# Up of a transformer block: one pair of output blocks by eight products instead of two, and three sums of h's blocks formed by GpSimd

## The chip, the cores and the metric

The kernel runs on one core of one Trainium2 chip. The metric is the device time of one execution in microseconds. Of the engines of the core, PE is TensorE (matmuls; PEld its weight loads), DVE is VectorE, ACT is ScalarE, POOL is GpSimd, and SP is the engine whose queue issues most loads. Each engine works through its own instructions in the order in which they stand, and waits for others through semaphores.

## The reference: what is computed

One block of a transformer on 512 tokens of width 2048, all in float32:

```
h = modulate(rms_norm(x, norm_mix), sh_a, sc_a)
...                                    # convolution and attention give y_conv, y_attn
x = x + g_a * (concat([y_conv, y_attn]) @ w_out)
h = modulate(rms_norm(x, norm_ffn), sh_f, sc_f)
x = x + g_f * ((silu(h @ ffn_w1) * (h @ ffn_w3)) @ ffn_w2)
```

The change lies in the last line: `h @ ffn_w1` and `h @ ffn_w3` (the weights are 2048 x 5632 each) are called Up here, the product with `ffn_w2` Down.

## The kernel before, in words

**Precision.** A float32 product is made of parts: a value is rounded to a high part (`hi`, type fp32r), and the rest is its low part (`lo`). Weights are split by a cast on ACT (`w_hi`, L1295) and a subtraction on DVE (`w_lo`, L1301). The blocks of h are split in the same way by `h_parts` (L1179 on ACT, L1180 on DVE); high and low half stand side by side in a tile `hC`, so that one matmul of 512 columns multiplies the weights' high part with both (L1309), and one of 256 columns adds the weights' low part times h's high part (L1310). `product` is eight such pairs of matmuls, one for each 128 rows of a half of the width.

**Pairs and products.** Up goes through 44 pairs u of output blocks: 128 columns of `ffn_w1` and the same of `ffn_w3`, each cut in an upper and a lower half of the width. A pair has four weight blocks of 128 x 1024: 11 and 21 of `ffn_w1`, 12 and 22 of `ffn_w3`. h is cut in four blocks `A[i, j]` of 128 x 2048 (i the half of the tokens, j the half of the width). A plain pair multiplies every weight block with two blocks of h: four steps, eight products (`plain_steps`, hC1 to hC4 for A[0,0], A[0,1], A[1,0], A[1,1]). All further pairs use a form of Strassen's scheme (`strassen_steps`): seven products, 1 to 7, of sums of weight blocks with sums of blocks of h. Product 1 takes weight block 11 with hC1, 5 takes 11 + 12 with hC5 (A[1,1] - A[1,0]), 2 takes 21 with hC2, 6 takes 11 + 12 + 22 with hC6, 3 takes 22 with a new hC3, 7 takes 12 + 22 with hC7 (A[0,0] - A[1,0]), 4 takes 21 + 11 + 12 + 22 with hC4. The weight sums are DVE additions (L1375 before, L1377 in the change, through `add`) and every product has its own split. The products gather in two banks of PSUM, x and y, and a third for product 2, and are read out by `take` (a copy on ACT and an addition on DVE, L1318 and L1319) and `more` (two additions on DVE, L1315). `PLAIN` pairs are plain, two of the 44 before. Product 4 of a pair is put behind the first two of the next pair; the first pair behind the plain ones has the order 1, 5, 2, 6, 3, 7, 4.

**The sums of blocks of h.** `h_sums(step)` is called once in each step n as long as n < 4 * PLAIN. Before, it forms the four sums on DVE at steps 1 to 4 (L1324, L1327, L1330, L1333) and splits them by `h_parts`; the plain pairs need none of them except that the old hC3 must be done with before the new is written (step 7). The sums are formed in place: A[1,1] becomes A[1,1] - A[1,0], A[1,0] becomes A[0,0] - A[1,0], and so on.

**Order.** The lists of steps are written out in `order`; a scheduler then places the instructions on the engines, so the order on an engine is not that of the code. The loop ahead of each step prepares later ones: a weight sum three steps ahead (`lead`), a split two steps ahead, the loads of a pair five steps ahead (`begin`). Loads of a pair go to the ring `raw` of four buffers when u <= PLAIN or u is a multiple of three, else to two buffers of `xy` (L1282). The four A blocks hold the four buffers of `xy`; they come free when the last reader of a block is done.

**Before and behind.** The end of the product with `w_out` gives x's second half late: A[1,0] and A[1,1] are made (`modulated`, L1191 on PE, L1195 on ACT) when the first three half steps of pair 0 are done. From step 8 * PLAIN on `gate_steps` runs beside the products: it loads rows of `ada_w`, scales them on ACT and adds them up by GpSimd's DMA queue. Down starts when Up is through; GpSimd stores each pair's result to DRAM (`store`), and Down reads them.

Of the kernel before, what the change touches and what calls it, by code (L numbers as in the profile page):

```python
# [10 lines left out]
F32 = mybir.dt.float32  # L11
# [3 lines left out]
ALU = mybir.AluOpType  # L15
# [5 lines left out]
S = 512  # L21
# [51 lines left out]
def block_kernel(ctx: ExitStack, tc: tile.TileContext, a: dict, out: bass.AP):  # L73
    nc = tc.nc
# [4 lines left out]
    def pool(name, bufs=1, stack=ctx, **kw):  # L79
        return stack.enter_context(tc.tile_pool(name=name, bufs=bufs, reuse_waits="tile", **kw))  # L80
# [443 lines left out]
    for k0 in range(0, KC, STEP):  # L524
        n = 12 if k0 == 0 else 9
# [61 lines left out]
    for name, m, t0, t1, n in (("q", 0, 0, NT, P), ("c", 1, NT, NT + 1, NP_), ("s", 2, 0, NT, P), ("w", 3, 0, NT, P)):  # L587
        f = SCALE if name == "q" else 1.0
        for h in range(2):
# [6 lines left out]
                                           op0=ALU.mult, op1=ALU.mult)  # L596
# [383 lines left out]
    HS, HK = S // 2, KC // 2  # L980
# [137 lines left out]
    A = {}  # L1118
# [3 lines left out]
    hC = {1: hc1.tile([P, HK, S], F32R, name="hC1")}  # L1122
# [44 lines left out]
    def row_norms(h):  # L1167

        r2 = rs2[:, 2 * h:2 * h + 2]
        nc.vector.reduce_sum(r2, ss2[:, 2 * h:2 * h + 2, :], axis=AX)  # L1170
        rsqrt(r2, r2, D)
        for e in range(2):
            dgs[h, e] = yp.tile([P, P], F32, tag="dn", name="dn", bufs=2)
            nc.vector.tensor_scalar(dgs[h, e], ident, rs2[:, 2 * h + e:2 * h + e + 1], None, op0=ALU.mult)

    def h_parts(p, src, k0, n):

        hi, lo = hC[p][:, k0:k0 + n, 0:HS], hC[p][:, k0:k0 + n, HS:S]
        nc.scalar.copy(hi, src)  # L1179
        nc.vector.tensor_sub(lo, src, hi.bitcast(F32))  # L1180
# [91 lines left out]
        for t in made:  # L1272
            x2_store(*t)
    row_norms(1)
    PLAIN = 2
    NU = FF // P

    def blocks(u):

        b = {}  # L1280
        for q, w, r0 in ((11, w1, 0), (21, w1, HK), (12, w3, 0), (22, w3, HK)):
            if u <= PLAIN or u % 3 == 0:  # L1282
                b[q] = ring[0].tile([P, HK * P], F32, tag="raw", name="raw")
# [37 lines left out]
    def h_sums(step):  # L1321

        if step == 1:
            nc.vector.tensor_sub(A[1, 1], A[1, 1], A[1, 0])  # L1324
            h_parts(5, A[1, 1], 0, HK)
        elif step == 2:
            nc.vector.tensor_sub(A[1, 0], A[0, 0], A[1, 0])  # L1327
            h_parts(7, A[1, 0], 0, HK)
        elif step == 3:
            nc.vector.scalar_tensor_tensor(A[0, 0], A[1, 1], -1.0, A[0, 0], op0=ALU.mult, op1=ALU.subtract)  # L1330
            h_parts(6, A[0, 0], 0, HK)
        elif step == 4:
            nc.vector.scalar_tensor_tensor(A[0, 1], A[0, 0], -1.0, A[0, 1], op0=ALU.mult, op1=ALU.subtract)  # L1333
        elif step == 4 * PLAIN - 1:
            h_parts(3, A[0, 1], 0, HK)

    def store(f, g):
        nc.gpsimd.dma_start(gd[f], g)
# [1 line left out]
    def plain_steps(u):  # L1340
        o = {}
        h = [slice(0, HS), slice(HS, S)]

        def make(q, w, j):
            def prep(s):
                s["hi"] = w_hi(o["b"][q])

            def mm(s, halves=(0, 1)):
                if j == 0 and 0 in halves:
                    o[w] = [(main, aux)[w]() for _ in range(2)]  # L1350
                for i in halves:
                    product(o[w][i], (s["hi"], s["lo"]), 1 + 2 * i + j, j == 0, j == 1)

            def post(s):
                if j == 0:
                    return
                d = o[f"d{w}"] = dp.tile([P, S], F32, tag=f"d{w + 1}", name=f"d{w + 1}")
                for i in range(2):
                    take(d[:, h[i]], o[w][i])
                if w == 0:  # L1360
                    nc.scalar.activation(d, d, AF.Silu)
                else:
                    nc.vector.tensor_mul(d, d, o["d0"])
                    store(u, d)

            return {"p": 0, "u": u, "o": o, "sum": lambda: None, "hi": prep, "src": q, "mm": mm, "post": post}

        return [make(q, w, j) for q, w, j in ((11, 0, 0), (21, 0, 1), (12, 1, 0), (22, 1, 1))]
# [68 lines left out]
    for u in range(NU):  # L1437
        new = plain_steps(u) if u < PLAIN else strassen_steps(u)
        if u == 0:
            new[1:3] = new[2], new[1]  # L1440
        if u == PLAIN:
            new[2:5] = new[4], new[2], new[3]
        order += new[:2]
        if late:
            order.append(late)
            late = None
        if u < PLAIN:
            order += new[2:]
# [8 lines left out]
    def begin(u):  # L1457
        if u < NU and u not in begun:
            begun.add(u)
            got = blocks(u)  # L1460
            for s in order:
                if s["u"] == u:
                    s["o"]["b"] = got
    def prepare(n, what):
        if n >= len(order):
            return
        s = order[n]
        if what == "sum":
            begin(s["u"])
            s["sum"]()  # L1470
        else:
            s["hi"](s)
            s["lo"] = w_lo(s["o"]["b"][s["src"]], s["hi"])
# [28 lines left out]
    def load_g(to, j, b, k):  # L1502
        to[b, k] = rings_g[j].tile([P, S], F32, tag=f"g{j}", name=f"g{j}", bufs=GM + 1)
        (nc.sync if b else nc.gpsimd).dma_start(to[b, k], gd[GROUPS[b][j][k]])
# [3 lines left out]
    for n, s in enumerate(order):  # L1508
        for m in range(n + 5, n + 1, -1):
            if m < len(order) and lead[id(order[m])] == m - n:  # L1510
                prepare(m, "sum")
        if n + 5 < len(order):
            begin(order[n + 5]["u"])
        if n > 2:
            prepare(n + 2, "split")
        if n < 4 * PLAIN:
            h_sums(n)
        s["mm"](s, (1,) if n < 3 else (0, 1)) if n < 4 * PLAIN else s["mm"](s)
        if 0 < n < 3:
            prepare(n + 2, "split")  # L1520
        s["post"](s)
        if n >= 8 * PLAIN:
            next(gate, None)
        if n == last_1:
            hst.close()
            rings_g[0] = pool("gtop", 1, side="right")
            for early in range(1, GM + 1):
                load_g(G0, 0, 0, early - 1)
# [91 lines left out]
```

## Time and profile before

| what | value |
|---|---|
| time, median of 3 runs | 2157.0 us (2156.54 to 2158.15) |
| the profiled execution | 2156.57 us |
| its span | 2154.8 us |
| Up's first product starts | 856.86 us into the span |
| Up's products with the whole of h begin | 873.07 us |
| the second pair begins | 887.33 us |
| the last weight load of L1309 | 1729.2 us |

Times in a timeline are us from the start of the span; a row has the start, the duration, the engine, the source line, what is written from what, and the shape. Where several equal instructions stand in a row, the duration is that of all of them together. Matmuls overlap: their own durations are longer than the distance between two starts, so a product is measured from start to start. `idle before` in brackets is how long the engine waited ahead of the row, and for whom.

### The profile page before, as it was taken

What the parts mean: (1) busy time and instruction counts of PE and PEld (TensorE: products, weight loads), DVE (VectorE), ACT (ScalarE), POOL (GpSimd) and SP (SyncE); (2) the same over time, 40 slices, a digit from 0 to 9 for tenths busy, and PEclk for the clock granted to TensorE, in tenths of its full rate; (3) what the DMA queues carried; (4) which work ended last, traced back from release to release, by engine and by line L of the source; (5) the groups of instructions that cost most, each with busy time, mean ns of one, the idle gap of its engine ahead of it and who ended that gap; (6) DMA issues with size and microseconds to landing.
All of it is one profiled execution on the core that took longest, in us unless ns stands there. A gap on an engine that the chain in (4) does not pass through costs nothing.

```text
span 2154.8 us, 30665 instructions
## 1 busy us (share of the span) xinstructions
PE 2125.5 (99%) x11011; PEld 1775.8 (82%) x11011; DVE 1780.1 (83%) x2776; ACT 1077.8 (50%) x1795; POOL 251.9 (12%) x336
## 2 busy tenths in 40 slices
PE   7999999999999999999999999999999999999998
PEld 5678778778788878888888888888888888888887
DVE  4998778878778789888888888888888877777888
ACT  5334345554442556655555555555555455554543
POOL 1110000000000233001100110110110140212032
PEclk9999999999999999999999999999999999999999
DMA  9984776545557999546666665665665499998897
GB/s 334 359 288 137 225 234 193 167 140 153 156 153 238 267 197 236 157 118 169 168 169 171 180 167 161 166 174 146 175 170 148 167 242 282 216 247 192 221 186 181
DMA packets 384778, 422.91 MB, mean 196 GB/s; under 512 B 21881, under 2 KB 293793, under 8 KB 383857
## 3 DMA queue, kind: packets, MB, share of 16 engines
q1 hardware_dynamic: 343216, 296.58, 44.5%
q0 software_dynamic: 41264, 124.23, 26.5%
q8 instruction: 87, 1.43, 0.3%
q14 instruction: 67, 0.54, 0.1%
q10 hardware_dynamic: 144, 0.13, 0.0%
HBM read 385.20 MB, written 19.94 MB: 188 GB/s over the span
## 4 chain that ended last, share of the span: by engine, by line
PE 87%; DVE 5%; DMA 5%; issue 2%; POOL 1%; ACT 0%; SPq 0%; DVEq 0%; POOLq 0%; ACTq 0%
PE main L1309 15%; PE main L1084 12%; PE aux L1084 12%; PE aux L1309 11%; PE main L1310 8%; PE aux L1310 6%; PE main L115 4%; PE main L117 4%; PE main L116 4%; DMA araw<-in_ada_w 3%; PE aux L888 2%; PE aux L860 2%; PE aux L115 1%; DMA t<-in_w_out 1%; PE aux L117 1%
## 5 line engine op out<-in xcount | busy, mean ns | idle before, releaser
L1309 PE MATMUL main<-hC,whi 128*128 128x512 f32 x1408 | 494.6, 393 | 0.0
L1310 PE MATMUL main<-hC,wlo 128*128 128x256 f32 x1408 | 394.4, 280 | 0.0
L1309 PE MATMUL aux<-hC,whi 128*128 128x512 f32 x1072 | 377.1, 392 | 0.0
L1309 PEld LDWEIGHTS main<-hC,whi 128*128 128x128 f32 x1408 | 263.6, 187 | 59.3 <-DVE hC L1180 0.3
L1310 PE MATMUL aux<-hC,wlo 128*128 128x256 f32 x1072 | 300.6, 280 | 0.0
L1310 PEld LDWEIGHTS main<-hC,wlo 128*128 128x128 f32 x1408 | 266.0, 189 | 0.0
L1309 PEld LDWEIGHTS aux<-hC,whi 128*128 128x128 f32 x1072 | 200.8, 187 | 44.8
L1301 DVE TENSOR_TENSOR wlo<-xy,whi 128x1024 fp32r<-128x1024 f32 x135 | 164.6, 1220 | 62.5 <-ACT whi L1295 62.5
L1310 PEld LDWEIGHTS aux<-hC,wlo 128*128 128x128 f32 x1072 | 202.6, 189 | 0.3 <-DVE wlo L1301 0.2
L1295 ACT CAST whi<-xy 128x1024 fp32r<-128x1024 f32 x135 | 142.3, 1054 | 104.6 <-issue 48.6
L1084 PE MATMUL aux<-wlo,phi 128*128 128x512 f32 (+1 forms) x422 | 164.4, 390 | 0.9 <-DVE wlo L1029 0.9
L1084 PE MATMUL main<-wlo,phi 128*128 128x512 f32 x420 | 163.7, 391 | 1.2 <-DVE wlo L1029 0.8
L1084 PE MATMUL aux<-whi,plo 128*128 128x512 f32 (+1 forms) x422 | 163.8, 388 | 0.0
L1084 PE MATMUL aux<-whi,phi 128*128 128x512 f32 (+1 forms) x422 | 163.6, 388 | 0.0
L1084 PE MATMUL main<-whi,plo 128*128 128x512 f32 x420 | 163.5, 389 | 0.0
L1084 PE MATMUL main<-whi,phi 128*128 128x512 f32 x420 | 163.5, 389 | 0.0
L1295 ACT CAST whi<-t 128x1024 fp32r<-128x1024 f32 x84 | 88.6, 1055 | 137.0 <-PE main L1309 64.3
L115 PE MATMUL main<-alo,whi 128*128 128x512 f32 x384 | 155.5, 405 | 0.0
L117 PE MATMUL main<-ahi,whi 128*128 128x512 f32 x384 | 151.4, 395 | 0.0
L116 PE MATMUL main<-ahi,wlo 128*128 128x512 f32 x384 | 150.6, 392 | 0.0
L1027 ACT CAST whi<-raw 128x1024 fp32r<-128x1024 f32 x90 | 94.7, 1054 | 111.1 <-PE aux L1084 37.8
L1027 ACT CAST whi<-xy 128x1024 fp32r<-128x1024 f32 x88 | 92.8, 1054 | 112.0 <-issue 41.1
(353 smaller groups left out, 4443.7 us busy)
## 6 DMA issues: line engine op xcount, KB each, us to landing
xy<-in_ffn_w SPq DMA_DIRECT2D x130, 512.0 KB, 4.8
raw<-in_ffn_w SPq DMA_DIRECT2D x107, 512.0 KB, 4.7
araw<-in_ada_w SPq DMA_DIRECT2D x208, 256.0 KB, 5.3
xy<-in_ffn_w POOLq DMA_DIRECT2D x66, 512.0 KB, 9.0
raw<-in_w_in SPq DMA_DIRECT2D x128, 192.0 KB, 3.2
xy<-in_ada_w SPq DMA_DIRECT2D x80, 256.0 KB, 4.0
graw<-in_ada_w SPq DMA_DIRECT2D x60, 256.0 KB, 2.8
acc<-graw POOLq DMA_DIRECT2D x60, 256.0 KB, 3.8
```

Of the source, the lines that this page charges most:

```text
L115: nc.tensor.matmul(ps, lhs[0], rhs[1], start=first, stop=False)
L116: nc.tensor.matmul(ps, lhs[1], rhs[0], start=False, stop=False)
L117: nc.tensor.matmul(ps, lhs[0], rhs[0], start=False, stop=last)
L860: nc.tensor.matmul(one[b], queries(g, i, h), kT[b][g][:, :L], start=True, stop=True)
L888: nc.tensor.matmul(po[:, b * HD:(b + 1) * HD], s["pT"][b][:, kb * P:(kb + 1) * P], vv[b][:, kb, g * HD:(g + 1) * HD], start=kb == 0, stop= ...
L1027: nc.scalar.copy(hi, wt)
L1084: nc.tensor.matmul(ps[:, q:q + wide], at_k[l][:, tok], wt[r][:, cs], start=begins and m == 0, stop=ends_ and j == i and m == 2, skip_group ...
L1295: nc.scalar.copy(hi, t)
L1301: nc.vector.tensor_sub(lo, t, hi.bitcast(F32))
L1309: nc.tensor.matmul(ps, wt[0][:, ks[k]], hC[p][:, k, :], start=first and k == 0, stop=False, skip_group_check=True)
L1310: nc.tensor.matmul(ps[:, HS:], wt[1][:, ks[k]], hC[p][:, k, 0:HS], start=False, stop=last and k == HK - 1, skip_group_check=True)
```

## The change

`PLAIN` goes from 2 to 1: pair 1 is now made of seven products instead of eight, in the order 1, 5, 2, 6, 3, 7, 4, and all later pairs move up. Since the products of pair 1 need sums of blocks of h, these are formed earlier and elsewhere: the first stays on DVE, the other three are formed by GpSimd at step 1, one behind the other. The signs change: A[0,0] becomes A[0,0] + A[1,1] (without the minus), and hC6 takes the minus when it is split, by ACT (L1332) and DVE (L1333). The splits of hC6, hC3 and hC7 are asked for at steps 4, 5 and 6. Pair 2 loads into buffers of `xy`, since u <= PLAIN no longer holds for it.

```diff
@@ -1272,7 +1272,7 @@
         for t in made:
             x2_store(*t)
     row_norms(1)
-    PLAIN = 2
+    PLAIN = 1
     NU = FF // P
 
     def blocks(u):
@@ -1322,17 +1322,19 @@
 
         if step == 1:
             nc.vector.tensor_sub(A[1, 1], A[1, 1], A[1, 0])
+            nc.gpsimd.tensor_sub(A[1, 0], A[0, 0], A[1, 0])
+            nc.gpsimd.tensor_add(A[0, 0], A[0, 0], A[1, 1])
+            nc.gpsimd.tensor_sub(A[0, 1], A[0, 0], A[0, 1])
+        elif step == 2:
             h_parts(5, A[1, 1], 0, HK)
-        elif step == 2:
-            nc.vector.tensor_sub(A[1, 0], A[0, 0], A[1, 0])
+        elif step == 4:
+            hi, lo = hC[6][:, :, 0:HS], hC[6][:, :, HS:S]
+            nc.scalar.mul(hi, A[0, 0], -1.0)
+            nc.vector.scalar_tensor_tensor(lo, A[0, 0], -1.0, hi.bitcast(F32), op0=ALU.mult, op1=ALU.subtract)
+        elif step == 5:
+            h_parts(3, A[0, 1], 0, HK)
+        elif step == 6:
             h_parts(7, A[1, 0], 0, HK)
-        elif step == 3:
-            nc.vector.scalar_tensor_tensor(A[0, 0], A[1, 1], -1.0, A[0, 0], op0=ALU.mult, op1=ALU.subtract)
-            h_parts(6, A[0, 0], 0, HK)
-        elif step == 4:
-            nc.vector.scalar_tensor_tensor(A[0, 1], A[0, 0], -1.0, A[0, 1], op0=ALU.mult, op1=ALU.subtract)
-        elif step == 4 * PLAIN - 1:
-            h_parts(3, A[0, 1], 0, HK)
 
     def store(f, g):
         nc.gpsimd.dma_start(gd[f], g)
@@ -1513,7 +1515,7 @@
             begin(order[n + 5]["u"])
         if n > 2:
             prepare(n + 2, "split")
-        if n < 4 * PLAIN:
+        if n <= 4 * PLAIN + 2:
             h_sums(n)
         s["mm"](s, (1,) if n < 3 else (0, 1)) if n < 4 * PLAIN else s["mm"](s)
         if 0 < n < 3:
```

How the instructions move, at three places. Names: `xy_7824` is A[0,0], `xy_7907` A[0,1], `xy_8040` A[1,0] and `xy_7940` A[1,1]; `raw_8120`, `raw_8122`, `raw_8124`, `raw_8126` are blocks 11, 21, 12 and 22 of pair 1, `whi` and `wlo` the parts of weights, `t2` a weight sum, `main_7988`, `main_7989`, `aux_8006`, `aux_8007` the banks of pair 0, `d1` and `d2` the results read from banks.

DVE from the first sum of h on, before (pair 1 is plain there):

```order
L1324 TENSOR_TENSOR xy_7940<-xy_7940,xy_8040 128x2048
L1319 TENSOR_TENSOR d1_8190<-main_7988,d1_8190 128x256
L1327 TENSOR_TENSOR xy_8040<-xy_7824,xy_8040 128x2048
L1180 TENSOR_TENSOR hC5_7906<-xy_7940,hC5_7906 128x8x256
L1180 TENSOR_TENSOR hC7_8110<-xy_8040,hC7_8110 128x8x256
L1319 TENSOR_TENSOR d1_8190<-main_7989,d1_8190 128x256
L1301 TENSOR_TENSOR wlo_8206<-raw_8122,whi_8204 128x1024
L1330 SCALAR_TENSOR_TENSOR xy_7824<-xy_7940,xy_7824 128x2048
L1319 TENSOR_TENSOR d2_8243<-aux_8006,d2_8243 128x256
L1319 TENSOR_TENSOR d2_8243<-aux_8007,d2_8243 128x256
L1301 TENSOR_TENSOR wlo_8252<-raw_8124,whi_8250 128x1024
L1363 TENSOR_TENSOR d2_8243<-d2_8243,d1_8190 128x512
```

and in the change:

```order
L1324 TENSOR_TENSOR xy_7940<-xy_7940,xy_8040 128x2048
L1319 TENSOR_TENSOR d1_8192<-main_7988,d1_8192 128x256
L1319 TENSOR_TENSOR d1_8192<-main_7989,d1_8192 128x256
L1301 TENSOR_TENSOR wlo_8200<-t2_8168,whi_8198 128x1024
L1377 TENSOR_TENSOR raw_8124<-raw_8124,raw_8126 128x1024
L1180 TENSOR_TENSOR hC5_7906<-xy_7940,hC5_7906 128x8x256
L1319 TENSOR_TENSOR d2_8234<-aux_8006,d2_8234 128x256
L1319 TENSOR_TENSOR d2_8234<-aux_8007,d2_8234 128x256
L1377 TENSOR_TENSOR t2_8168<-t2_8168,raw_8126 128x1024
L1365 TENSOR_TENSOR d2_8234<-d2_8234,d1_8192 128x512
L1301 TENSOR_TENSOR wlo_8244<-raw_8122,whi_8242 128x1024
L1333 SCALAR_TENSOR_TENSOR hC6_8109<-xy_7824,hC6_8109 128x8x256
```

The sums of h on L1327 and L1330 are gone from DVE; in their place stand the weight sums (L1377) of pair 1, and hC5 comes two rows later than before. The rows of the change go on up to the low part of product 7's weights (`wlo_8330`), with `main_8248` and `aux_8280` the x and y bank of pair 1 and `aux_8307` that of its product 2:

```order
L1333 SCALAR_TENSOR_TENSOR hC6_8109<-xy_7824,hC6_8109 128x8x256
L1319 TENSOR_TENSOR d1_8265<-main_8248,d1_8265 128x256
L1301 TENSOR_TENSOR wlo_8276<-t2_8168,whi_8274 128x1024
L1180 TENSOR_TENSOR hC3_7904<-xy_7907,hC3_7904 128x8x256
L1319 TENSOR_TENSOR d2_8297<-aux_8280,d2_8297 128x256
L1301 TENSOR_TENSOR wlo_8303<-raw_8126,whi_8301 128x1024
L1180 TENSOR_TENSOR hC7_8110<-xy_8040,hC7_8110 128x8x256
L1315 TENSOR_TENSOR d1_8265<-aux_8307,d1_8265 128x256
L1377 TENSOR_TENSOR raw_8122<-raw_8122,t2_8168 128x1024
L1315 TENSOR_TENSOR d1_8265<-aux_8307,d1_8265 128x256
L1301 TENSOR_TENSOR wlo_8330<-raw_8124,whi_8328 128x1024
L1319 TENSOR_TENSOR d2_8297<-main_8248,d2_8297 128x256
```

Before, hC7 stood next to hC5, hC6 and the new hC3 stood among the splits of pair 1's plain steps; now hC6, hC3 and hC7 each stand between the splits of the products that need them.

POOL behind the last stores of x, before:

```order
L1163 DMA xd0_6358<-y2_6435 128x512
L1163 DMA xd1_6359<-y2_6435 128x512
L1338 DMA gd0_6362<-d2_8243 128x512
L1338 DMA gd1_6363<-d2_8409 128x512
L1338 DMA gd2_6364<-d2_8470 128x512
```

and in the change:

```order
L1163 DMA xd1_6359<-y2_6435 128x512
L1325 ISA
L1325 TENSOR_TENSOR xy_8040<-xy_7824,xy_8040 128x2048
L1326 TENSOR_TENSOR xy_7824<-xy_7824,xy_7940 128x2048
L1327 TENSOR_TENSOR xy_7907<-xy_7824,xy_7907 128x2048
L1340 DMA gd0_6362<-d2_8234 128x512
```

The three sums, and one ISA instruction that the build sets ahead of them, now stand between the last store of x and the first store of a pair. The first sum waits for DVE's L1324.

PE in the second pair of the change, at the end of product 6 and the start of product 3:

```order
L1310 MATMUL main_8248<-hC6_8109,wlo_8276 128x256
L1309 MATMUL aux_8280<-hC3_7904,whi_8301 128x512
L1309 MATMUL main_8403<-hC1_6409,whi_8352 128x512
L1310 MATMUL aux_8280<-hC3_7904,wlo_8303 128x256
L1309 MATMUL aux_8280<-hC3_7904,whi_8301 128x512
L1310 MATMUL aux_8280<-hC3_7904,wlo_8303 128x256
```

The first matmul of product 1 of pair 2 (`main_8403`, weights `whi_8352` from the third pair's load `xy_8268`) stands between the first two of product 3. The loads of `xy_8268` and `xy_8271` go into the buffers of A[1,1] and A[0,0] and wait on the SP queue for DVE and for the second and the third sum on POOL.

## The prediction

> **What bounds the kernel now.** I read the page first, then busy time by stretch, then what TensorE's weight loads waited for, and last the timelines of TensorE, VectorE and ScalarE at the start of Up. The page:
>
> ```profile
> span 2154.8 us, 30665 instructions
> PE 2125.5 (99%) x11011; PEld 1775.8 (82%) x11011; DVE 1780.1 (83%) x2776; ACT 1077.8 (50%) x1795; POOL 251.9 (12%) x336
> ```
>
> TensorE is busy 99% of the span. Such a share is an average, so here are the stretches of Up (us of busy time, instructions in brackets); the plain pairs lie in the first and the start of the second:
>
> ```profile
> core 0: us, PE busy (x) PEld busy (x) DVE busy (x) ACT busy (x) POOL busy (x), PEclk, DMA share, GB/s
> 873.00:900.00 27.00, 27.00 (x156) 23.55 (x156) 24.14 (x19) 20.55 (x27) 0.54 (x1) 1.00 0.41 120
> 900.00:960.00 60.00, 60.00 (x347) 52.76 (x346) 52.91 (x65) 28.57 (x41) 2.53 (x4) 1.00 0.54 162
> 960.00:1700.00 740.00, 740.00 (x4263) 650.84 (x4262) 634.74 (x843) 386.42 (x556) 72.60 (x97) 1.00 0.61 166
> ```
>
> TensorE has no free time in them, at a granted clock of 1.00, and VectorE is next, busy 24.14 of 27.00 us. What the weight loads waited for from 873 us to the end:
>
> ```profile
> engine line waited for: us in total, times, longest us
> PEld main L1084 <- issue: 0.4, 1, 0.4
> PEld aux L1310 <- DVE wlo L1301: 0.2, 1, 0.2
> ```
>
> So behind 873 us TensorE waits 0.6 us in all. Nothing later can swallow a delay, or a gain: what TensorE loses or saves at the start of Up arrives at the end of the program in full.
>
> **The product that is saved.** Starts on TensorE (start, duration), the first of a product, the first of the next, and the first of the second pair:
>
> ```profile
> 876.03 0.40 PE L1309 MATMUL aux<-hC,whi 128*128 128x512 f32 x1
> ...
> 878.86 0.40 PE L1309 MATMUL main<-hC,whi 128*128 128x512 f32 x1
> ...
> 887.33 0.39 PE L1309 MATMUL main<-hC,whi 128*128 128x512 f32 x1
> ```
>
> Durations overlap, so the price of a product is the distance of starts: 878.86 - 876.03 = 2.83 us for eight matmuls of 512 columns and eight of 256. The order has 9916 rows on TensorE before and 9900 now, 16 fewer: one product. The change does what it says, and its whole gain is 2.83 us, 0.13% of 2157 us. A difference of 0.2%, 4.3 us, is about what a measurement of this kernel can tell from no change, so even the undisturbed gain lies below that. The question is what the second pair now waits for.
>
> It begins at 887.33 as before, and without waits its products would begin at 2.83 us apart: 1 at 887.33, 5 at 890.16, 2 at 892.99, 6 at 895.82, 3 at 898.65, 7 at 901.48 (901.7 with the early matmul of the third pair's first product, 0.23 us, which the order now sets inside product 3). Before, eight plain products, 22.6 us, lay between 887.33 and the first product that needs hC5, and nobody waited for the sums. Now product 5 needs hC5 2.83 us after the pair begins, and 6, the new 3 and 7 follow at once.
>
> **What VectorE has to do in that time.** Its rows of before give the distances from start to start of each kind of operation:
>
> ```profile
> 878.32 1.23 DVE L1301 TENSOR_TENSOR wlo<-raw,whi 128x1024 fp32r<-128x1024 f32 x1 [1.09 <-ACT whi L1295]
> ...
> 881.73 2.29 DVE L1324 TENSOR_TENSOR xy<-xy 128x2048 f32<-128x2048 f32 x1
> 883.93 0.42 DVE L1319 TENSOR_TENSOR d<-main,d 128x256 f32<-128x256 f32 x1
> 884.27 2.28 DVE L1327 TENSOR_TENSOR xy<-xy 128x2048 f32<-128x2048 f32 x1
> 886.47 4.49 DVE L1180 TENSOR_TENSOR hC<-xy,hC 128x2048 fp32r<-128x2048 f32 x2
> 890.87 0.42 DVE L1319 TENSOR_TENSOR d<-main,d 128x256 f32<-128x256 f32 x1
> 891.20 1.22 DVE L1301 TENSOR_TENSOR wlo<-raw,whi 128x1024 fp32r<-128x1024 f32 x1
> 892.34 2.28 DVE L1330 SCALAR_TENSOR_TENSOR xy<-xy 128x2048 f32<-128x2048 f32 x1
> ...
> 896.34 0.68 DVE L1363 TENSOR_TENSOR d<-d,d 128x512 f32<-128x512 f32 x1
> 896.94 2.28 DVE L1180 TENSOR_TENSOR hC<-xy,hC 128x2048 fp32r<-128x2048 f32 x1
> ```
>
> That is 2.20 us for 128x2048 (4.40 for the two at 886.47), 1.14 for 128x1024, 0.60 for 128x512 and 0.34 for a 128x256 out of PSUM. Three sums of 2.20 leave VectorE (6.6 us), but the pair's weight sums (1.14 each) and its splits for every product come in. The first weight sum stands ahead of hC4 in the order and falls into the idle time there (1.09 us ahead of 878.32, and the like before it), so I cost it at nothing; without that cover it costs 1.14. Then, in the order shown, from the end of L1324 at 883.93: two takes 0.68, low part of the weight sum 1.14, weight sum for product 7 1.14, low half of hC5 2.20 (ends 889.1), two takes 0.68, weight sum for 6 1.14, d2 times d1 0.60, low part for 2 1.14 (892.7), low half of hC6 2.20 (894.9), take 0.34, low part for 6 1.14 (896.3), low half of hC3 2.20 (898.5), take 0.34, low part for 3 1.14, low half of hC7 2.20, 0.34, weight sum for 4 1.14, 0.34, low part for 7 1.14. Together 21.24 us: product 7 can begin at 905.2. Against 901.7 that is a wait of 3.5 us, with VectorE never held up by anybody. So the gain is already spent: -2.8 + 3.5 = +0.7 us. The margin at product 5 is 890.16 - 889.1 = 1 us, at product 2 0.3 us: whatever holds VectorE up beyond that, TensorE waits for.
>
> **What GpSimd brings.** Of before there are only these rows to price a sum on it from:
>
> ```profile
> L547 POOL MEMSET v<- 128x512 f32 x2 | 1.1, 526 | 25.4 <-DVE wlo L109 19.2 <-issue 6.2
> L1608 POOL MEMSET const-uint8-127<- 128x1 uint8 x1 | 0.1, 98 | 0.0
> ```
>
> (526 - 98) / 511 = 0.84 ns for each further element that is written; 2048 elements are 1.7 us a stream. A sum has two streams in and one out: 1.8 us if all go at once, 3.5 if two follow one another, 5.25 if all three do. I take T = 4.4, midway between the last two, since the only row shows one stream alone at 0.84 ns; 1.8 to 5.25 stay for the range. [...]
>
> The first sum waits for L1324, so it starts at about 884.1. GpSimd is free by then, as its row of before tells (idle 42.27 us ahead of 897.32, that is from 855.05):
>
> ```profile
> 897.32 0.54 POOL L1338 DMA_DIRECT2D gd<-d  x1 [42.27 <-DVE d L1363]
> ```
>
> The ISA row that the order now has ahead of it can use these 29 us, so I cost it at nothing; if it needs longer, each us of it delays the sums by one. The store of pair 0 is queued behind the three sums on GpSimd; its receiver is far off (Down), so it costs nothing. The weight loads of the third pair go into the buffers of A[1,1] and A[0,0] on the SP queue, behind the second and the third sum:
>
> ```profile
> raw<-in_ffn_w SPq DMA_DIRECT2D x4, 512.0 KB, 5.1
> xy<-in_ffn_w SPq DMA_DIRECT2D x4, 512.0 KB, 6.8
> ```
>
> At 6.8 us a landing they are there by about 907 in the forecast below, for a product that begins behind product 7, after 917; nothing. The load for 7's weight sum goes at 879.5 (end of the row at 878.32) and lands 5.1 later, at 884.6; needed at 885.8.
>
> **Do the two engines hinder each other?** No row of before shows GpSimd and VectorE reading SBUF at once. So bounds: nothing, or each sum keeps VectorE from starting any operation with two operands in SBUF for its whole length, 3 x T. Nearly all rows of the chain above are of that kind (all but the takes), and they run end to end at 1.1 ns an element (1.14 us for 1024) with no slot left over for a partner, if a path is shared. I take the upper end: the first sum begins while VectorE does the two takes (0.68 us, out of PSUM), which hides 0.5 us of it, and 883.93 + 21.24 + 3 x 4.4 - 0.5 = 917.9. Product 7 waits 917.9 - 901.7 = 16.2 us in all (most of it shows already at product 5, which waits for hC5), less 2.83: **+13.4 us**. T of 3.5 gives +10.7, 5.25 gives +15.9.
>
> [...]
>
> **Rivals.** (a) The engines run beside each other undisturbed. Then the second sum ends at 884.1 + 8.8 + 0.2 for the handover = 893.1, the third at 897.6. ScalarE's high half takes 1.82:
>
> ```profile
> 884.05 1.92 ACT L1179 CAST hC<-xy 128x2048 fp32r<-128x2048 f32 x1 [0.39 <-DVE xy L1324]
> 885.87 0.36 ACT L1318 COPY d<-aux 128x256 f32<-128x256 f32 x1
> ```
>
> so hC3's high half is there at 899.4, its low half at 901.6, and the 6.64 us that VectorE still has in front of product 7 end at 908.2: a wait of 6.5, +3.7 us, 2160.7. With T = 5.25 it is +6.3. For it: that no row shows such a hindrance. Against it: nothing but the argument on the slots.
> (b) Not slower: the sums on GpSimd are short and disturb nobody. The second must end 1.82 before VectorE comes to hC6 at 892.65 and the third 1.82 before 896.3, so from T of 3.2 down only VectorE's own chain counts: +0.7 us, 2157.7, no difference that can be told. For it: 1.8 us lies within the bounds. Against it: that all three streams would have to run at the pace of one.
> (c) Faster by over 0.2% would need more than the product is worth; I see no way.
>
> **How the numbers follow.** The profiled execution took 2156.57 us (span 2154.8 and 1.8 around it), 0.4 less than the median of 2157.0; 2156.57 + 13.4 = 2170.0, and put on the median 2170.4. Chances: hindrance 0.55, (a) 0.27, (b) 0.15, and 0.03 for what I do not see. Slower by over 0.2% are all of the first and nearly half of (a) (T over 4.6, or a late first sum), 0.12, and a bit of the rest: 0.68. Within 0.2%: the rest of (a), and (b): 0.30. Faster 0.02. The likeliest case alone spans 2164 (T of 2.3, as on VectorE) to 2173. The range has to take in (a) from 2158.2 (T = 3.5) on and leaves out (b): 2158 to 2175, the upper end by T = 5.25 and 2 us for a late first sum.
>
> **What would show it.** In the trace of the change: three GpSimd rows of L1325 to L1327 of about 4.4 us each from 884 on; VectorE rows with two SBUF operands that start at the end of one of them or last far longer than 1.22 and 2.28 us, while takes keep 0.42; TensorE waiting for hC5 at about 890 for some 12 us, and 16 in all by product 7, and none after it. If VectorE's rows keep their length and start as before beside the sums, the hindrance is wrong; if TensorE waits first at hC6 (from 895.8), it is (a); if only at product 7, (b). The forecast is wrong altogether if TensorE's starts from product 1 to 7 stay 2.83 apart.

## The result, and the profile after

| what | before | after |
|---|---|---|
| time, median of 6 runs each | 2157.96 us (2156.54 to 2160.68) | 2174.32 us (2172.99 to 2177.35) |
| ratio after to before, 95% interval | | 1.0077 [1.0067, 1.0087] |
| the profiled execution, its span | 2156.57, 2154.8 us | 2172.99, 2171.1 us |
| Up, from its first product to Down's first weight load | 872.65 us | 887.01 us |

Slower by 16.4 us; the forecast was 2170.4, in a range of 2158 to 2175. Of the 16.3 us between the two spans, 14.4 lie in Up, 0.5 ahead of it (where the change does nothing) and 1.5 at the very end. Down itself is as long as before, 419.26 us from its first weight load to its last matmul in both, but the last store of the output is issued 3.62 us behind that matmul instead of 2.12. The page of the change:

```profile
span 2171.1 us, 30673 instructions
PE 2126.4 (98%) x10995; PEld 1774.7 (82%) x10995; DVE 1795.5 (83%) x2786; ACT 1080.7 (50%) x1799; POOL 267.3 (12%) x339
```

TensorE has 16 matmuls fewer (11011 before), GpSimd and VectorE are busy 15 us longer each. Busy time by stretch shows where, with the columns as in the prediction:

```profile
873.00:900.00 27.00, 17.62 (x104) 15.16 (x102) 24.82 (x12) 16.71 (x23) 15.23 (x3) 0.88 0.14 39
900.00:960.00 60.00, 55.38 (x303) 48.06 (x304) 56.06 (x68) 30.20 (x40) 4.44 (x7) 0.94 0.71 202
960.00:1700.00 740.00, 740.00 (x4262) 650.76 (x4261) 634.39 (x842) 384.81 (x553) 71.34 (x96) 1.00 0.60 162
```

TensorE stands idle 9.4 of the first 27 us and 4.6 of the next 60, and never after. VectorE is as busy in the first stretch as before (24.8 against 24.1 us), but with 12 instructions instead of 19: each lasts longer. What the weight loads waited for from 873 us on (us in total, times, longest):

```profile
PEld aux L1309 <- DVE hC L1180: 12.0, 1, 12.0
PEld main L1309 <- DVE d L1319: 1.8, 1, 1.8
PEld main L1309 <- ACT whi L1295: 1.1, 1, 1.1
```

One wait of 12 us for hC5, and 2.9 us behind it. GpSimd's three sums:

```profile
884.61 4.63 POOL L1325 TENSOR_TENSOR xy<-xy 128x2048 f32<-128x2048 f32 x1 [29.11 <-DVE xy L1324]
889.32 5.37 POOL L1326 TENSOR_TENSOR xy<-xy 128x2048 f32<-128x2048 f32 x1
894.77 5.36 POOL L1327 TENSOR_TENSOR xy<-xy 128x2048 f32<-128x2048 f32 x1
```

And VectorE's timeline in the same time, the rows to lay beside them:

```profile
884.38 0.75 DVE L1319 TENSOR_TENSOR d<-main,d 128x256 f32<-128x256 f32 x2
885.05 5.28 DVE L1301 TENSOR_TENSOR wlo<-t,whi 128x1024 fp32r<-128x1024 f32 x1
890.25 5.52 DVE L1377 TENSOR_TENSOR raw<-raw 128x1024 f32<-128x1024 f32 x1
895.70 6.58 DVE L1180 TENSOR_TENSOR hC<-xy,hC 128x2048 fp32r<-128x2048 f32 x1
902.20 0.74 DVE L1319 TENSOR_TENSOR d<-aux,d 128x256 f32<-128x256 f32 x2
902.87 1.21 DVE L1377 TENSOR_TENSOR t<-t,raw 128x1024 f32<-128x1024 f32 x1
```

Read the ends. The first sum ends at 889.24; the low part that began at 885.05 ends 1.09 behind it, at 890.33, about its own length. The second sum, begun at 889.32, ends at 894.69, 4.36 behind that end; VectorE's next operation ends 1.08 behind the sum. Each row holds the wait for the other engine and then its own work: the engines take turns, one whole operation each. The takes, with one operand in PSUM, pass in 0.75 for two (884.38 to 885.13, the sum from 884.61 on). When the third sum is over, a 128x1024 is back at 1.21. The three rows are 4.06, 4.30 and 4.30 us longer than 1.22, 1.22 and 2.28: 12.66 us lost.

TensorE's product 5 and product 7:

```profile
902.34 0.79 PE L1309 MATMUL aux<-hC,whi 128*128 128x512 f32 x1 [11.72 <-DVE hC L1180]
...
903.14 0.63 PE L1309 MATMUL aux<-hC,whi 128*128 128x512 f32 x1
903.57 0.41 PE L1310 MATMUL aux<-hC,wlo 128*128 128x256 f32 x1
903.78 0.63 PE L1309 MATMUL aux<-hC,whi 128*128 128x512 f32 x1
...
918.68 0.50 PE L1309 MATMUL main<-hC,whi 128*128 128x512 f32 x1 [1.50 <-DVE d L1319]
```

Behind the 12 us a pair of matmuls takes 0.64 us (903.14 to 903.78) instead of 0.35. Product 7 starts at 918.68, 61.36 us behind Up's first product; without waits it would be 901.7 - 856.86 = 44.84, so it is 16.5 late. Behind the wait the granted clock (third figure from the right: 0.69, 0.50, 0.86) had fallen:

```profile
887.80:902.50 14.70, 2.98 (x18) 2.35 (x17) 14.70 (x4) 4.21 (x6) 12.17 (x3) 0.69 0.00 0
902.50:906.00 3.50, 3.50 (x11) 3.02 (x12) 3.50 (x6) 1.83 (x2) 0.56 (x1) 0.50 0.69 205
906.00:910.00 4.00, 4.00 (x21) 3.46 (x21) 4.00 (x4) 3.41 (x4) 0.00 (x0) 0.86 0.59 188
```

### The profile page after: what moved, and what is told of

The parts are those of the page before. It is cut to its first block, busy times and chain, and to the rows that moved or that the text cites. A ratio compares the mean times of both kernels' runs of the same rounds, so it can differ in the third digit from the quotient of the medians.

```text
span 2171.1 us, 30673 instructions
## 1 busy us (share of the span) xinstructions
PE 2126.4 (98%) x10995; PEld 1774.7 (82%) x10995; DVE 1795.5 (83%) x2786; ACT 1080.7 (50%) x1799; POOL 267.3 (12%) x339
## 4 chain that ended last, share of the span: by engine, by line
PE 85%; DMA 6%; DVE 4%; issue 2%; ACT 1%; POOL 1%; SPq 0%; POOLq 0%; DVEq 0%; ACTq 0%
PE main L1309 14%; PE aux L1309 11%; PE main L1084 10%; PE aux L1084 10%; PE main L1310 7%; PE aux L1310 6%; PE main L115 5%; PE main L117 5%; PE main L116 5%; DMA araw<-in_ada_w 2%; DMA t<-in_w_out 2%; PE aux L888 2%; PE aux L860 2%; DMA raw<-in_w_out 1%; PE aux L115 1%
## 5 line engine op out<-in xcount | busy, mean ns | idle before, releaser
L1309 PE MATMUL aux<-hC,whi 128*128 128x512 f32 x1064 | 376.2, 394 | 11.7 <-DVE hC L1180 11.7
L1301 DVE TENSOR_TENSOR wlo<-xy,whi 128x1024 fp32r<-128x1024 f32 x140 | 170.5, 1218 | 64.5 <-ACT whi L1295 64.5
L1295 ACT CAST whi<-xy 128x1024 fp32r<-128x1024 f32 x140 | 147.4, 1053 | 113.0 <-issue 52.8
L1027 ACT CAST whi<-xy 128x1024 fp32r<-128x1024 f32 x88 | 92.7, 1054 | 111.5 <-issue 41.1
```

Source lines behind the costliest of these rows:

```text
L1027: nc.scalar.copy(hi, wt)
L1295: nc.scalar.copy(hi, t)
L1301: nc.vector.tensor_sub(lo, t, hi.bitcast(F32))
L1309: nc.tensor.matmul(ps, wt[0][:, ks[k]], hC[p][:, k, :], start=first and k == 0, stop=False, skip_group_check=True)
```

## The experiments

The theory to be tested (**hindrance**): a GpSimd sum and a VectorE operation with two operands in SBUF exclude each other, so every sum costs VectorE its own length. The rival (**late results**): they run side by side, and TensorE waits because the results come late. The kernels without sums, and those in which GpSimd's work is not read, leave the sums of h out of what Up computes. Up begins at another time in each profiled execution (856.9 to 860.7 us), so the places below count from Up's first product. "Lost" is by how much VectorE's rows are longer than in the run without sums, with operations that are added to it (for the early unread sum the 2.77 us by which L1324 comes later, for the fills an idle time of 1.03); "Up" is Up's length against the 872.65 us of before.

| kernel | time against before, median | product 7 starts | later than without sums | VectorE lost | Up |
|---|---|---|---|---|---|
| the change | +16.4 | 61.36 | 12.67 | 12.66 | +14.4 |
| without sums, two times | +4.0, +3.4 | 48.68, 48.69 | 0 | 0 | +3.2, +2.0 |
| without sums, the wait filled | +4.1 | 48.69 | 0 | 0 | +2.8 |
| unread sums, first early | +15.3 | 60.17 | 11.48 | 11.49 | +14.7 |
| unread sums, all late | +16.7 | 60.80 | 12.11 | 12.10 | +14.1 |
| unread copies | +7.3 | 52.76 | 4.07 | 4.09 | +7.6 |
| unread fills | +5.8 | 49.89 | 1.20 | 1.03 | +4.7 |
| all sums on VectorE | +9.7 | 55.29 | 6.60 | 6.60 | +8.6 |
| one sum on GpSimd | +12.3 | 57.17 | 8.48 | 8.46 | +10.5 |
| sums in quarters | +18.7 | 63.05 | 14.36 | | +16.2 |
| second pair plain | +6.5 | | | | +7.7 |

**Without sums.** From the change:

```diff
-            nc.gpsimd.tensor_sub(A[1, 0], A[0, 0], A[1, 0])
-            nc.gpsimd.tensor_add(A[0, 0], A[0, 0], A[1, 1])
-            nc.gpsimd.tensor_sub(A[0, 1], A[0, 0], A[0, 1])
```

> The change with the three sums on GpSimd left out: hC6, hC3 and hC7 are split from the blocks A[0,0], A[0,1] and A[1,0] as they stand, so a part of what Up computes is left out. GpSimd has nothing to do here, so this is VectorE's chain by itself. All theories: 21.24 us from the end of L1324, product 7 some 3.5 us late, one product (2.83 us) fewer: +0.7 us against the kernel before, 0 to +2. If it is slower by over 5 us, the sums are not the cause and something else in the change is.

Measured: 2162.11 us against 2158.14, ratio 1.0021 [1.0012, 1.0031]. GpSimd does nothing here, and 12.7 of the 16.5 us by which product 7 was late are gone. The scheduler now sets the low half of hC6 (L1330) ahead of that of hC5 on VectorE; up to product 7 the operations are the same ones, so the length of the chain can be compared. Product 7 starts 48.68 us behind Up's first product; the forecast for VectorE's chain alone was 905.2 - 856.86 = 48.34. The 0.34 more is one take: product 7 goes on in the bank from which product 6 is read, and that read (L1319 of main) stands behind product 7's low part. But the time was to be +0.7, 0 to +2 at most, and is +4.0. TensorE around product 7:

```profile
906.37 0.40 PE L1309 MATMUL main<-hC,whi 128*128 128x512 f32 x1
909.15 0.51 PE L1309 MATMUL main<-hC,whi 128*128 128x512 f32 x1 [2.38 <-DVE d L1319]
...
910.02 0.63 PE L1309 MATMUL main<-hC,whi 128*128 128x512 f32 x1
...
910.66 0.63 PE L1309 MATMUL main<-hC,whi 128*128 128x512 f32 x1
```

After 2.38 us of idle time the matmuls go at 0.64 us a pair from 910.0 to 913.3, at a granted clock of 0.50: some 1.7 us for which nobody is waited for. The waits of the weight loads are 4.4 us in this stretch (2.7 for that take, 1.7 for low parts); 4.4 + 1.7 - 2.8 for the product saved = 3.3, and Up is 3.2 longer. The same kernel, run a second time:

> The run without sums once more, the same kernel, as the partner of the next one on the same chip: +4 us against the kernel before, a wait of 2.7 us for product 7 and behind it some 3 us at a granted clock of 0.50.

```profile
906.34 0.50 PE L1309 MATMUL main<-hC,whi 128*128 128x512 f32 x1 [2.41 <-DVE d L1319]
...
908.20 0.40 PE L1309 MATMUL main<-hC,whi 128*128 128x512 f32 x1
...
908.57 0.40 PE L1309 MATMUL main<-hC,whi 128*128 128x512 f32 x1
```

The same wait, and against the expectation no fall: 0.35 us a pair, Up +2.0 instead of +3.2; the times are 2160.82 against 2157.47, 1.0014 [1.0005, 1.0024]. So a wait of 2.4 us was followed by a clock of 0.50 in one execution and of 1.00 in another.

**The wait filled with work.** Six pairs of product 3 done twice:

```diff
-                product(o[bank], (s["hi"], s["lo"]), p, first, last)
+                product(o[bank], (s["hi"], s["lo"]), p, first, last and (u, p) != (PLAIN, 3))
+                if (u, p) == (PLAIN, 3):
+                    for k in range(2, HK):
...
```

> As the run without sums, but product 3 of the second pair is 14 pairs of matmuls long instead of 8: the last six are done twice, so its sum is another. That is 2.1 us more work for TensorE, at the place where it waits 2.7 us for product 7. If the fall of the granted clock comes from that wait: no fall, and product 7 and what follows at 0.35 us a pair; 1.7 us less than the run without sums, although TensorE does more. If the clock falls for another reason (the long waits earlier, chance): the same time as without the filling, or 2 us more.

2161.55 us, 1.0014 [1.0005, 1.0023]: the time of the second run without sums within 0.8 us, with 2.1 us more work on TensorE and product 7 at 48.69 again. Up is 0.8 us longer than there, and a row of the gate (L223) waits 0.9 us. The clock does not fall, but in the second run without sums it did not either, so this does not decide what the fall comes from. It shows that the 2.1 us do not move product 7, since VectorE is last there.

**Unread sums.** The three sums write into the still empty tile of hC7:

```diff
-            nc.gpsimd.tensor_sub(A[1, 0], A[0, 0], A[1, 0])
-            nc.gpsimd.tensor_add(A[0, 0], A[0, 0], A[1, 1])
-            nc.gpsimd.tensor_sub(A[0, 1], A[0, 0], A[0, 1])
+            free = hC[7][:, :, 0:HS]
+            nc.gpsimd.tensor_sub(free, A[0, 0], A[1, 0])
+            nc.gpsimd.tensor_add(free, A[0, 0], A[1, 1])
+            nc.gpsimd.tensor_sub(free, A[0, 0], A[0, 1])
```

> As the run without sums, but GpSimd forms three sums of the same size from the same blocks and writes them into the still empty tile of hC7, where nobody reads them (what is computed is that of the run without sums). Nobody waits for a result of GpSimd, so only the hindrance of VectorE is left. Hindrance: VectorE loses three sums of 4.6 to 4.7 us, product 7 starts at about 918, +13 us against the kernel before (+12 to +16). Undisturbed side by side, with late results as the cause: the same as the run without sums, +0.7 us.

2173.41 us, 1.0071 [1.0055, 1.0088], as the hindrance was to give (+12 to +16). The first sum did not need L1324 and ran ahead of it, so L1324 itself came 2.77 us later; the other two lengthened two rows by 4.42 and 4.30. Together 11.49, and product 7 is 11.48 later than without sums. With all three held back to behind L1324 (each reads A[1,1]):

> As the first run with unread sums, but each of the three reads A[1,1], so that none can start before L1324 is done, as in the change. Hindrance: VectorE loses three whole sums behind L1324, TensorE waits for hC5 and then up to product 7, which starts 61 us behind the first product of Up, as in the change (48.7 without sums): +14 to +17 us against the kernel before. Undisturbed: the time of the run without sums, +4.

2174.17 us, 1.0072 [1.0057, 1.0087], the time of the change. VectorE's and GpSimd's timelines:

```profile
887.10 6.68 DVE L1180 TENSOR_TENSOR hC<-xy,hC 128x2048 fp32r<-128x2048 f32 x1
893.71 0.41 DVE L1319 TENSOR_TENSOR d<-main,d 128x256 f32<-128x256 f32 x1
894.04 5.20 DVE L1301 TENSOR_TENSOR wlo<-t,whi 128x1024 fp32r<-128x1024 f32 x1
...
899.83 4.93 DVE L1378 TENSOR_TENSOR t<-t,raw 128x1024 f32<-128x1024 f32 x1
```

```profile
884.88 6.76 POOL L1326 TENSOR_TENSOR hC<-xy 128x2048 fp32r<-128x2048 f32 x1 [29.20 <-ACT hC L1179]
891.72 6.45 POOL L1327 TENSOR_TENSOR hC<-xy 128x2048 fp32r<-128x2048 f32 x1
898.24 5.44 POOL L1328 TENSOR_TENSOR hC<-xy 128x2048 fp32r<-128x2048 f32 x1
```

4.40 + 3.98 + 3.72 = 12.1 us lost, product 7 is 12.1 later, and the take at 893.71 keeps its 0.41 beside a sum. Nobody reads these sums. One engine does wait for GpSimd, against the expectation: ScalarE has to write the real hC7 over them:

```profile
903.71 1.90 ACT L1179 CAST hC<-xy 128x2048 fp32r<-128x2048 f32 x1 [8.66 <-POOL hC L1328]
```

That wait delays nothing here, since VectorE goes from row to row without idle time from L1324 up to product 7, and its longer rows alone make the 12.1 us. Late results are refuted as the cause.

**Unread copies and fills.** In place of the sums three copies with one input, or (behind a copy of one column, to hold them back) three fills:

```diff
+            nc.gpsimd.tensor_copy(free, A[1, 1])
+            nc.gpsimd.tensor_copy(free, A[0, 0])
+            nc.gpsimd.tensor_copy(free, A[0, 1])
```

> As the run with unread sums, but three copies of 128x2048 with one input on GpSimd instead of the sums. Hindrance by anything that reads SBUF on GpSimd: VectorE's rows with two SBUF operands wait for each copy, three times the copy's own length. If only operations with two SBUF inputs take turns: VectorE's rows keep 1.22 and 2.28 us and the time is that of the run without sums, +0.7 us. Undisturbed: the same +0.7.

2165.41 us, 1.0034 [1.0021, 1.0047]. The copies also take turns with VectorE. Its rows and GpSimd's:

```profile
887.49 3.98 DVE L1180 TENSOR_TENSOR hC<-xy,hC 128x2048 fp32r<-128x2048 f32 x1
...
891.73 2.57 DVE L1301 TENSOR_TENSOR wlo<-t,whi 128x1024 fp32r<-128x1024 f32 x1
```

```profile
885.26 4.06 POOL L1326 CAST hC<-xy 128x2048 fp32r<-128x2048 f32 x1 [29.18 <-ACT hC L1179]
889.38 3.84 POOL L1327 CAST hC<-xy 128x2048 fp32r<-128x2048 f32 x1
```

The first copy ends at 889.32, 1.8 us after VectorE's row before it let it go (887.49); VectorE's split, begun at 887.49, ends at 891.47, 2.15 behind the copy. A copy takes 1.8 us of its own, and three of them lengthen VectorE's rows by 1.70, 1.36 and 1.03, 4.09 in all.

> As the run with unread sums, but behind a copy of a single column, which holds GpSimd back until L1324 is done, three fills of 128x2048 that read nothing. From 0.84 ns an element they last 1.8 us each, 5.4 together. If reading by GpSimd is what hinders: VectorE's rows keep their length, +0.7 us. If any use of SBUF by GpSimd hinders: up to 5.4 us more, +6.

2163.89 us, 1.0030 [1.0019, 1.0041]. VectorE's rows and GpSimd's, and the waits of ScalarE and VectorE behind them:

```profile
885.43 2.28 DVE L1334 SCALAR_TENSOR_TENSOR hC<-xy,hC 128x2048 fp32r<-128x2048 f32 x1
887.63 2.29 DVE L1180 TENSOR_TENSOR hC<-xy,hC 128x2048 fp32r<-128x2048 f32 x1
```

```profile
885.41 2.35 POOL L1326 CAST hC<-xy 128x1 fp32r<-128x1 f32 x1 [29.19 <-ACT hC L1179]
887.82 5.55 POOL L1328 MEMSET hC<- 128x2048 f32 x3
```

```profile
893.40 1.91 ACT L1179 CAST hC<-xy 128x2048 fp32r<-128x2048 f32 x1 [1.38 <-POOL hC L1328]
896.28 1.23 DVE L1301 TENSOR_TENSOR wlo<-t,whi 128x1024 fp32r<-128x1024 f32 x1 [1.03 <-ACT whi L1295]
```

The fills, 1.85 us each, run through VectorE's rows from 887.6 to 893.4, and these keep 1.21 and 2.29. The copy of a single column, which reads, lasted 2.35: it stood behind the 2.28 of L1334. So, of what was tried, the GpSimd operations that read, sums and copies, held up VectorE's rows (by 3.61 to 4.43 and by 1.03 to 1.70 us each), and the fills, which only write, didn't. The 1.2 us by which product 7 is late have another cause, again the wait for the tile: ScalarE waited 1.38 us for the fills before it could write hC7, and VectorE 1.03 for ScalarE.

**All sums on VectorE; one sum on GpSimd.** The three operations on `nc.vector`; then the first of them back on GpSimd:

```diff
-            nc.gpsimd.tensor_sub(A[1, 0], A[0, 0], A[1, 0])
-            nc.gpsimd.tensor_add(A[0, 0], A[0, 0], A[1, 1])
-            nc.gpsimd.tensor_sub(A[0, 1], A[0, 0], A[0, 1])
+            nc.vector.tensor_sub(A[1, 0], A[0, 0], A[1, 0])
+            nc.vector.tensor_add(A[0, 0], A[0, 0], A[1, 1])
+            nc.vector.tensor_sub(A[0, 1], A[0, 0], A[0, 1])
```

> The change with the three sums on VectorE instead of GpSimd, same order of products. VectorE's chain gets three operations of 2.20 us more: 21.24 + 6.6 = 27.8 us, product 7 can start at 911.8, a wait of 10.1 us, less 2.83: +7.3 us against the kernel before, in every theory. Hindrance: so it is faster than the change by some 8 us, because a sum on GpSimd costs VectorE more than the sum itself would. Undisturbed: the change should have been the faster of the two; its time would have to come from elsewhere.

> The change with only the first of the three sums on GpSimd and the other two on VectorE. Hindrance: VectorE's chain has 21.24 + 4.4 of its own and loses 4.6 less 0.5 to the one sum: product 7 at about 913.7, +9 us against the kernel before, between all on VectorE (+7.3) and all on GpSimd (+16). Undisturbed: 21.24 + 4.4, product 7 at 909.6, +5 us, less than all on VectorE.

2167.94 us, 1.0044 [1.0030, 1.0058], and 2170.58, 1.0055 [1.0039, 1.0070]. VectorE's chain is as long as forecast: three sums of 2.20 move product 7 by 6.60, one on GpSimd and two on VectorE by 4.06 + 4.40 = 8.46 (measured 8.48). So the sum on GpSimd cost VectorE nearly twice (4.06) what the sum itself would (2.20). Both times are 2.4 and 3.3 us above the expectation; TensorE in the first:

```profile
896.85 0.58 PE L1310 MATMUL aux<-hC,wlo 128*128 128x256 f32 x1 [3.91 <-DVE wlo L1301]
897.23 0.63 PE L1309 MATMUL aux<-hC,whi 128*128 128x512 f32 x1
...
914.33 0.50 PE L1309 MATMUL main<-hC,whi 128*128 128x512 f32 x1 [2.38 <-DVE d L1319]
```

Behind the 3.9 us the clock is at half (0.50 up to 902.5), behind the 2.38 it is not (1.00); the first is hidden, since VectorE is last again at product 7. Of the 2.4 us, 0.3 are the take, 0.9 come in Up behind product 7, and the rest lies outside Up or between this profile and the median.

**Sums in quarters.** Each sum as four operations of 128x512:

```diff
-            nc.gpsimd.tensor_sub(A[1, 0], A[0, 0], A[1, 0])
+            for k in (slice(k, k + 2) for k in range(0, HK, 2)):
+                nc.gpsimd.tensor_sub(A[1, 0][:, k], A[0, 0][:, k], A[1, 0][:, k])
...
```

> The change with each of the three sums cut into four operations of 128x512. Hindrance in turns: a VectorE operation waits for one quarter (1.2 us) instead of a whole sum, so hC5 is there after three or four quarters and product 5 starts at about 893 instead of 903; the total of VectorE and GpSimd time up to product 7 stays the same, so product 7 starts at 917 to 919 still and the time is that of the change, +14 to +17 us. If the long waits with their fall of the granted clock cost time of their own, it is less. Undisturbed: no difference between the two kernels at any product.

2176.95 us, 1.0082 [1.0069, 1.0096], above the +14 to +17 that was expected. Product 5 starts 35.28 us behind Up's first product instead of 45.02, as expected; but the long wait only moves. Four quarters now last 9.06 us, since VectorE gets its turn between them, so the sum for hC6 comes late, and VectorE waits for it through ScalarE. In this kernel late results do cost time:

```profile
888.01 9.06 POOL L1326 TENSOR_TENSOR xy<-xy 128x512 f32<-128x512 f32 x4 [29.12 <-DVE xy L1324]
...
904.39 8.01 POOL L1330 TENSOR_TENSOR xy<-xy 128x512 f32<-128x512 f32 x4
```

```profile
906.41 2.66 DVE L1336 SCALAR_TENSOR_TENSOR hC<-xy,hC 128x2048 fp32r<-128x2048 f32 x1 [4.34 <-ACT hC L1335]
```

**The second pair plain, sums still on GpSimd.** This takes only the other half of the change:

```diff
-    PLAIN = 1
+    PLAIN = 2
...
-        elif step == 5:
+        elif step == 7:
             h_parts(3, A[0, 1], 0, HK)
...
-        if n <= 4 * PLAIN + 2:
+        if n < 4 * PLAIN:
```

> The change with the second pair plain again (PLAIN = 2), the three sums still on GpSimd; the new hC3 is split at step 7, since the old one is needed until step 6. The sums of h now have the 22.6 us of eight plain products as cover. Hindrance: the first waits are not for hC5; but VectorE's splits for the plain steps lie behind the sums: low part of block 12 at about 902 instead of 898.7, so TensorE waits some 3 us there: +3 us against the kernel before (+1 to +4.5). Undisturbed: 6.6 us less work for VectorE and nobody waits: 0 (within 0.5).

2164.72 us, 1.0031 [1.0020, 1.0041]. The sums have 22.6 us of cover, and still cost 6.5 us:

```profile
884.61 5.29 DVE L1301 TENSOR_TENSOR wlo<-raw,whi 128x1024 fp32r<-128x1024 f32 x1
889.82 6.71 DVE L1180 TENSOR_TENSOR hC<-xy,hC 128x2048 fp32r<-128x2048 f32 x1
...
897.23 4.29 DVE L1365 TENSOR_TENSOR d<-d,d 128x512 f32<-128x512 f32 x1
901.45 1.21 DVE L1301 TENSOR_TENSOR wlo<-raw,whi 128x1024 fp32r<-128x1024 f32 x1
```

Again three rows lengthened (by 4.07, 4.43 and 3.61), and the low part of block 12 is there at 902.7: the expected wait, 4.1 us by the weight loads. The expectation of +3 (+1 to +4.5) left out the fall of the clock behind it (0.50 from 904 on, 1.7 us) and later waits. The waits for low parts in that bank are 4.7 in all, those for further low parts, takes and the gate's rows 1.7: 4.7 + 1.7 + 1.7 = 8.1, against 7.7 in Up.

None of these beats the kernel before. The whole gain is one product, 2.8 us; already with no sums at all product 7 waits longer than that.

## Why the forecast held, and where it was short

- **One product saved.** Shown: 16 matmuls fewer. Products before stand 2.79 apart on average (four from 887.33 to 898.49), so 2.83 was right within 0.04.
- **TensorE bound behind 873 us, every delay passes on.** Shown: in the stretch from 960 us on TensorE is busy all the time, and in every kernel whose product 7 is in the table, its delay, less the product saved, is still there at the end of Up. The first weight sum cost nothing, as assumed: L1324 starts 24.86 us behind Up's first product, 24.87 before.
- **VectorE's chain alone, product 7 3.5 us late.** 48.34 us forecast, 48.69 measured; the missing step is the take of product 6, 0.34. The length was right, its price on TensorE was not: +0.7 net is +2.0 without and +3.2 with a fall of the clock, +3.4 to +4.0 in the medians. The sum took each wait at its own length and no fall of the clock.
- **T = 4.4.** The first sum, which waited for nobody, shows 4.63; what a sum took from VectorE was 4.06 to 4.30 here. The value was good, the way to it was not: a copy, with one stream in and one out, takes 1.8 us, as a fill with one stream out does (1.85), so the copy's reading added nothing that shows to its writing, and two inputs one behind the other would by that estimate give 3.6. That the middle of two bounds came out right was luck.
- **The hindrance, 3 x 4.4 - 0.5 = 12.7.** 12.66 measured, and 12.1 with sums that nobody reads. That a sum holds up VectorE's operations with two operands in SBUF, for its whole length, was the author's assumption when the forecast was made. The runs show such rows 3.61 to 4.43 us longer by a sum and 1.03 to 1.70 by a copy, while rows beside fills keep 1.21 and 2.29 and a take beside a sum its 0.41. What the two engines share, and whether it is short of slots, no run shows.
- **The place and size of the waits.** Forecast: some 12 us for hC5 at about 890, none behind product 7. Shown: 12.0 us. Product 7 at 917.9 forecast, 918.68 measured; 0.46 of it is that Up began later in this execution, 0.34 the take. "16 in all by product 7" came out as 16.5, but not of waits alone: the matmuls stood idle for 14.0 us (11.72, 0.79 and 1.50), and some 2.3 us went to half clock at product 5. Without the fall TensorE would have waited those 2.3 us longer at product 7, since VectorE's chain decides when that starts.
- **The rivals.** (a), side by side with late results, is refuted by the unread sums; (b), short sums, by the row of 4.63 us. The ISA row cost nothing: the first sum starts 0.15 us behind the end of L1324 (882.18 + 2.28).
- **What is left.** The forecast was +13.4, the profiled execution shows +16.3. Of the 2.9 us, 0.3 are the take, 0.7 come in Up behind product 7, 0.5 lie ahead of Up and 1.5 behind Down's last matmul. Of the 0.7, 0.2 are that a product takes 2.79 and not 2.83; for the rest no wait accounts, and the other runs have up to 1 us like it. The last store is issued 2.0 to 4.1 us behind the last matmul in the other kernels: 2.0 and 2.1 with the wait filled and with the second pair plain, 3.0 to 4.1 in the rest. The medians of the kernels with seven products in the second pair lie between 0.3 us below and 2.6 above what Up shows. What delays the last store was not settled.

## What to carry to other kernels

Work moved from VectorE to GpSimd was no relief here: GpSimd read SBUF while VectorE's next operations had two operands there, and a sum that VectorE does in 2.2 us cost it 3.6 to 4.4 us, up to the whole length of GpSimd's operation. Fills on GpSimd, and VectorE's takes, with one operand in PSUM, showed no such loss. Look for it in the rows: an operation that has suddenly the length of two, ending its own length behind the end of the other engine's. And where TensorE is busy all the time, price a new wait with a possible stretch at half clock behind it (here it came behind a wait of 2.4 to 2.5 us in four of seven executions, for 3.3 to 3.5 us, which cost some 1.7), unless another engine decides when the next product can start.

## What the runs showed of the hardware

- **Whole operations in turn.** In the five kernels of the table with whole sums or copies on GpSimd for which VectorE's loss is given, that loss accounts for the shift of product 7 within 0.02 us. Next to nothing was lost in the change of hands: the sum that waited for nobody lasted 4.63 us, the two that had to wait ended 4.36 us behind VectorE's row.
- **The granted clock fell behind some waits.** A wait of 2.38 to 2.52 us for product 7 was followed by a granted clock of 0.50 in four profiled executions (without sums, the first unread sums, copies, fills) and not in three (without sums again, all on VectorE, one on GpSimd). The longer waits of these kernels in Up (2.8, 3.0 and 3.0 in the quarters and the late unread sums; 3.8, 3.9, 4.2, 4.7, 7.5, 11.7) all had it, save one of 3.0 with only two matmuls behind it, which cannot tell. Of the shorter ones, two had it (2.0 in the copies, 1.7 in the quarters), each with another wait just ahead, and those of 1.5, 1.6, 1.7, 1.8 and 2.2 in five kernels had not. TensorE then worked some 3 to 6.6 us at 0.50 (910.0 to 913.3 without sums, 909.5 to 916.1 in the quarters), which cost some 1.7 to 3.0. What decides whether the clock falls no run here shows.
- **In the change that fall was free:** 2.3 us at product 5, and product 7 still came when VectorE was ready.
